# A hybrid S5 and attention decoder block on one core: y matmuls with a full-width stationary operand, and GpSimd copies back to channel order

## The chip, the cores and the metric

The kernel runs on one core of a Trainium2 chip. Its time is the device time of one execution, in microseconds (us). TensorE (PE in the rows) multiplies matrices from SBUF into PSUM; VectorE (DVE), ScalarE (ACT) and GpSimd (POOL) work on elements; SyncE (SP) issues the weight loads. Each engine takes its instructions in a fixed order and waits on semaphores of the others.

## The reference, cut to what matters

One layer of a decoder block on 256 tokens of width 2048: adaptive modulation from `c`, RMSNorm, one projection to u, q, k, v, an S5 state space mixer on u, dilated attention on q, k, v, an output projection, and a SwiGLU block. The edited work is the end of the S5 mixer: 64 groups of 16 channels with 64 complex states each.

```python
def _s5_mixer(u, a_re, a_im, log_dt, b_re, b_im, c_re, c_im, d, w_glu):
    ...
    y = (jnp.einsum('sbgn,gcn->bsgc', h_re, c_re.astype(f32))
         - jnp.einsum('sbgn,gcn->bsgc', h_im, c_im.astype(f32))
         + d.astype(f32) * uf)
    y = jax.nn.gelu(y.reshape(B, S, SSM_WIDTH))
    return y * jax.nn.sigmoid(y @ w_glu.astype(f32))
```

## The kernel before, in words

All activations are kept as a high and a low part in fp32r, and most products are three matmuls (high x high, high x low, low x high). Weights stream through a ring: `load` (line 104) has SP issue a 512 KB DMA into one of six `raw` buffers, ScalarE rounds it to `whi` (line 131), VectorE subtracts to `wlo` (line 133), and there are three pairs of those (`NHL`). The order of the loads on SP is written out by hand (lines 110 to 118); the order of the other engines' instructions is set at compile time by a scheduler that goes by priorities and by times of its own.

The S5 mixer works on 256 tokens as 64 positions j of 4 phases r. `ssm_batch(m)` (line 689) does batch m, eight groups in four partition quarters Q, for m from 0 to 7. It multiplies U with the table `wv` into S (line 698), copies S to scratch (line 701), turns it with the tables `E`, scans it along time on VectorE (line 713), turns it back into the state `hp`, and then makes y from two tables: `T` (within four tokens, from U) and `Vt` (from `hp`). In the kernel before, y has channels of quarter Q on partitions 32Q to 32Q + 31 and the phases r beside each other; every matmul has a stationary operand of 128x32, set at column 32Q of the array (lines 725 to 733). GELU follows on ScalarE and VectorE (lines 735 to 743), and lines 744 to 747 write its high and low part to `yT`, block m.

Scratch comes from `WK`: tiles of 128x3x512 with two buffers, which `ssm_batch`, `ssm_rot` (`wkr`, line 475), `ssm_tables` (`wkt`, line 502) and every other head of attention (`wkh`, line 797) share. PSUM tiles of the tag `ms` have three buffers. The batches are generators in two lanes (lines 884 to 888), of which `step` (line 865) advances some between the half blocks of the q, k, v projection (lines 889 to 906); two batches thus go nearly together. The tables of batches 6 and 7 are made between batches 2, 3 and 4, 5. After the last batch the matmuls z (line 919) read `yT`, block by block from 0 to 7, while the heads of attention and the gate1 row (memset and DMA on GpSimd, lines 253 and 254; sums on VectorE, line 268) go on.

GpSimd does memsets for tables and a few DMAs, and nothing else.

Of the kernel before, what the change touches and what calls it, by code (L numbers as in the profile page):

```python
# [7 lines left out]
F32 = mybir.dt.float32  # L8
F32R = mybir.dt.float32r
I32 = mybir.dt.int32  # L10
AF = mybir.ActivationFunctionType
ALU = mybir.AluOpType
# [49 lines left out]
def body(tc, sm, tabs, bc, brow, x, wada, wg2, win, wglu, wout, wgate, wup, wdown, out):  # L62
    nc = tc.nc
    V, A, PE, G, SP = nc.vector, nc.scalar, nc.tensor, nc.gpsimd, nc.sync
# [13 lines left out]
    def ms(shape, name="ms"):  # L78
        return ms_p.tile(shape, F32, name=name, tag="ms", bufs=3)
# [81 lines left out]
    def WK(name):  # L161

        w = p2.tile([128, 3, 512], F32, name=name, tag="wk", bufs=2)

        def part(i, *shape):
            n = math.prod(shape)
            names = "abcd"[:len(shape)]
            v = w[:, i, 0:n]
            return v.rearrange(f"p ({' '.join(names)}) -> p {' '.join(names)}", **dict(zip(names, shape)))
        return part  # L170


# [167 lines left out]
    def tt(o, a, b, op):  # L340
        V.tensor_tensor(out=o, in0=a, in1=b, op=op)  # L341
    def ts(o, a, s1_, s2_, o0, o1=None):
        if o1 is None:
            V.tensor_scalar(out=o, in0=a, scalar1=s1_, scalar2=None, op0=o0)
        else:
            V.tensor_scalar(out=o, in0=a, scalar1=s1_, scalar2=s2_, op0=o0, op1=o1)
# [121 lines left out]
    def te_parts(m):  # L468

        te = te_p[m // 2]  # L470
        T = te[:, 512 * (m % 2):512 * (m % 2) + 512].rearrange("p (q r c) -> p q r c", q=4, r=4)
        E = te[:, 1024:2048].rearrange("p (e q j) -> p e q j", e=2, q=8)
        return T, E[:, :, 4 * (m % 2):4 * (m % 2) + 4]

    def ssm_rot(mp):

        if mp == 2:
            te = xp.tile([128, D], F32, name="te", tag="x", bufs=2)
        else:
            te = p2.tile([128, D], F32, name="te", tag="te", bufs=2)  # L480
        te_p[mp] = te
        E = te[:, 1024:2048].rearrange("p (e q j) -> p e q j", e=2, q=8)
        pr = slice(8 * mp, 8 * mp + 8)
        wk = WK("wkr")
        G.memset(E[:, 0, :, 0:1], 1.0)
        G.memset(E[:, 1, :, 0:1], 0.0)
        ea, eb = wk(0, 2, 8, 32), wk(1, 2, 8, 32)
        for l in range(6):
            n = 1 << l
            for dst, r in ((ea, 0), (eb, 1)):  # L490
                f = el[:, l, r, pr].unsqueeze(1).unsqueeze(3).to_broadcast([128, 2, 8, n])
                tt(dst[:, :, :, 0:n], E[:, :, :, 0:n], f, ALU.mult)
            tt(E[:, 0, :, n:2 * n], ea[:, 0, :, 0:n], eb[:, 1, :, 0:n], ALU.subtract)
            tt(E[:, 1, :, n:2 * n], ea[:, 1, :, 0:n], eb[:, 0, :, 0:n], ALU.add)
            if l == 3:
                yield 1.5
            elif l == 4:
                yield 1.2
        rot_done.add(mp)
        yield 2.2  # L500

    def ssm_tables(m):
# [7 lines left out]
        wv_t[m] = wv  # L510
        wst = T4([128, 4, 2, 4, 32], "wst")
        wk = WK("wkt")
        T, _ = te_parts(m)
        Tf = T.rearrange("p q r c -> p (q r c)")
# [132 lines left out]
    U = xp.tile([128, 8, 4, 64], F32, name="U", tag="x", bufs=2)  # L647
# [38 lines left out]
    yT = [P8([128, 4, 2, 256], f"yT{i}", F32R) for i in range(2)]  # L686


    def ssm_batch(m):
        while m // 2 not in rot_done:  # L690
            yield None
        wv = wv_t[m]
        Vt = wv[:, 1]
        T, E = te_parts(m)
        S = ms([128, 2, 4, 64], "S")
        for Q in range(4):
            for e in range(2):
                PE.matmul(S[:, e, Q], lhsT=wv[:, 0, Q, e].rearrange("p i c -> p (i c)"), rhs=U[:, m, Q], start=True, stop=True)  # L698
        wk = WK("wks")
        a, b, s = (wk(i, 2, 4, 64) for i in range(3))  # L700
        A.copy(s, S)
        yield 0.0
        Er = E[:, 0].unsqueeze(1).to_broadcast([128, 2, 4, 64])
        Ei = E[:, 1].unsqueeze(1).to_broadcast([128, 2, 4, 64])
        tt(a, s, Er, ALU.mult)
        tt(b, s, Ei, ALU.mult)
        tt(s[:, 0], a[:, 0], b[:, 1], ALU.add)
        tt(s[:, 1], a[:, 1], b[:, 0], ALU.subtract)
        yield 2.0
        g, a2, b2 = a, b, s  # L710
        for e in range(2):
            for Q in range(4):
                V.tensor_tensor_scan(out=g[:, e, Q], data0=rho4[:, 4 * m + Q:4 * m + Q + 1].to_broadcast([128, 64]), data1=s[:, e, Q],
                                     initial=0.0, op0=ALU.mult, op1=ALU.add)
        yield 1.1
        tt(a2, g, Er, ALU.mult)
        tt(b2, g, Ei, ALU.mult)
        hp = g
        V.memset(hp[:, :, :, 0:1], 0.0)
        tt(hp[:, 0, :, 1:64], a2[:, 0, :, 0:63], b2[:, 1, :, 0:63], ALU.subtract)  # L720
        tt(hp[:, 1, :, 1:64], a2[:, 1, :, 0:63], b2[:, 0, :, 0:63], ALU.add)
        yield 2.0
        yield None
        y = ms([128, 4, 64], "y")
        for Q in range(4):
            yq = y[32 * Q:32 * Q + 32]
            for r in range(4):
                PE.matmul(yq[:, r], lhsT=T[:, Q, r], rhs=U[:, m, Q], start=r == 0, stop=False, skip_group_check=True,  # L728
                          tile_position=(0, 32 * Q))
            for r in range(4):  # L730
                for e in range(2):
                    PE.matmul(yq[:, r], lhsT=Vt[:, Q, e, r], rhs=hp[:, e, Q], start=False, stop=e == 1, skip_group_check=True,  # L732
                              tile_position=(0, 32 * Q))

        ysb, t1 = wk(1, 64, 4), wk(2, 64, 4)
        A.copy(ysb, y.rearrange("p r j -> p j r"))
        A.activation(t1, ysb, AF.Square)
        yield 0.0
        ts(t1, t1, 0.044715, 1.0, ALU.mult, ALU.add)
        tt(t1, t1, ysb, ALU.mult)  # L740
        A.activation(t1, t1, AF.Tanh, scale=math.sqrt(2.0 / math.pi))
        yield 0.6
        V.scalar_tensor_tensor(out=ysb, in0=t1, scalar=1.0, in1=ysb, op0=ALU.add, op1=ALU.mult)
        dst = yT[m // 4][:, m % 4]
        yf = ysb.rearrange("p j r -> p (j r)")
        A.mul(dst[:, 0], yf, 0.5)
        V.scalar_tensor_tensor(out=dst[:, 1], in0=yf, scalar=0.5, in1=dst[:, 0].bitcast(F32), op0=ALU.mult, op1=ALU.subtract)
        done_b.add(m)
        yield 0.7

# [133 lines left out]
    for m in BO:  # L884
        lanes[m % 2].append(ssm_batch(m))
# [24 lines left out]
    for nb in range(2):  # L910
        z = acc([128, 4, 256], "z")
        for hf in range(4):
            hl = take()
            for j in range(2):
                kc = hf * 2 + j
                for c in range(4):
                    w = slice(c * 128, c * 128 + 128)
                    for n, (wt, a) in enumerate(((hl[0], 0), (hl[0], 1), (hl[1], 0))):
                        PE.matmul(z[:, c], lhsT=wt[:, j, w], rhs=yT[kc // 4][:, kc % 4, a], start=(kc == 0 and n == 0 and c % 2 == 0),  # L919
                                  stop=(kc == 7 and n == 2), skip_group_check=True)  # L920
# [317 lines left out]
```

## Time and profile before

| | |
|---|---|
| time, median of 3 runs | 1264.25 us (1263.53 to 1267.47) |
| profiled execution | 1264.14 us |
| its span, first to last instruction | 1262.4 us |
| TensorE busy | 1216.4 us (96%), 6884 matmuls |
| VectorE busy | 790.5 us (63%) |
| ScalarE busy | 570.5 us (45%) |
| GpSimd busy | 25.2 us (2%), 50 instructions |
| chain that ended last | TensorE 80%, VectorE 9%, DMA 6%, ScalarE 3% |
| HBM read and written | 299.44 and 2.10 MB, 239 GB/s over the span |

The profile is of one execution. Times in rows are us from the start of the span, durations of single instructions are in ns where a row says min/median/max or mean. L732 is line 732 of the kernel. TensorE's durations are modelled and overlap; the start of one instruction to the start of the next is its pace. "[0.37 <-DVE yT L747]" behind an instruction means that its engine sat idle for 0.37 us before it, until that line's instruction on VectorE had ended.

### The profile page before, as it was taken

To read this page: it belongs to the slowest core of one execution; us is meant where nothing else is said; L and a number is where in the kernel's file an instruction comes from. 1 tells how busy PE (TensorE), PEld (TensorE's weight loads), DVE (VectorE), ACT (ScalarE), POOL (GpSimd) and SP (SyncE) were. 2 spreads that over 40 slices of the span, in tenths; PEclk is the share of its full clock that TensorE was granted. 3 is DMA by queue.
4 is the path that set the end of the run, shared out by engine and by line. 5 is a ranking of instruction groups with operands and counts; after the bars stand their busy time and mean duration, and the time that the engine had idled before them with its cause. 6 is when DMAs were issued, how large, how long until landed. Compare 5 with 4: busy or idle time off the path is not lost.

```text
span 1262.4 us, 18076 instructions
## 1 busy us (share of the span) xinstructions
PE 1216.4 (96%) x6884; PEld 965.2 (76%) x6884; DVE 790.5 (63%) x1389; ACT 570.5 (45%) x859; POOL 25.2 (2%) x50
## 2 busy tenths in 40 slices
PE   4888999999999999999999999999999999999998
PEld 2555667677789877688888888888888878888886
DVE  7894356667778989865655665665555444545443
ACT  3564373445455554554444444444434443333432
POOL 0210000000000000000000000000000000000000
PEclk9899999999999999999999999999999999999999
DMA  8788886777687799567777777777766556667662
GB/s 338 275 285 319 318 318 239 262 251 272 221 322 237 266 317 330 202 188 241 237 238 235 230 239 240 238 236 229 244 201 191 185 169 194 208 194 213 190 212 68
DMA packets 83032, 302.74 MB, mean 240 GB/s; under 512 B 9248, under 2 KB 9664, under 8 KB 82304
## 3 DMA queue, kind: packets, MB, share of 16 engines
q1 hardware_dynamic: 80784, 294.69, 70.4%
q10 hardware_dynamic: 1728, 4.38, 0.9%
q0 software_dynamic: 432, 2.51, 0.5%
q8 instruction: 54, 0.88, 0.3%
q14 instruction: 34, 0.28, 0.1%
HBM read 299.44 MB, written 2.10 MB: 239 GB/s over the span
## 4 chain that ended last, share of the span: by engine, by line
PE 80%; DVE 9%; DMA 6%; ACT 3%; issue 2%; SPq 0%; DVEq 0%; ACTq 0%
PE ff L150 38%; PE dn L150 14%; PE qkv L150 8%; PE dnl L150 5%; DMA raw<-wada 3%; PE ada L231 3%; PE uacc L608 3%; DVE wlo L133 2%; PE y L732 2%; DMA raw<-win 1%; DVE gate L268 1%; PE q L150 1%; PE y L728 1%; PE z L919 1%; PE S L698 1%
## 5 line engine op out<-in xcount | busy, mean ns | idle before, releaser
L133 DVE TENSOR_TENSOR wlo<-raw,whi 128x1024 fp32r<-128x1024 f32 x365 | 445.7, 1223 | 325.8 <-ACT whi L131 325.0
L131 ACT CAST whi<-raw 128x1024 fp32r<-128x1024 f32 x365 | 384.4, 1053 | 511.1 <-PE ff L150 268.6
L150 PE MATMUL ff<-whi,h2T 128*128 128x512 f32 x1408 | 437.2, 390 | 0.7 <-DVE h2T L1034 0.5
L150 PEld LDWEIGHTS ff<-whi,h2T 128*128 128x128 f32 x1408 | 264.0, 188 | 56.8 <-DVE h2T L1034 0.9
L150 PE MATMUL ff<-wlo,h2T 128*128 128x512 f32 x704 | 274.1, 389 | 0.0
L150 PE MATMUL dn<-whi,aT 128*128 128x512 f32 x528 | 163.4, 390 | 0.0
L150 PEld LDWEIGHTS ff<-wlo,h2T 128*128 128x128 f32 x704 | 132.2, 188 | 27.1
L150 PEld LDWEIGHTS dn<-whi,aT 128*128 128x128 f32 x528 | 99.1, 188 | 21.1 <-ACT whi L131 0.2
L150 PE MATMUL qkv<-whi,hT 128*128 128x512 f32 x320 | 107.4, 402 | 0.1
L150 PE MATMUL dn<-wlo,aT 128*128 128x512 f32 x264 | 103.1, 391 | 0.0
L231 PE MATMUL ada<-raw,c 128*4 128x256 f32 (+1 forms) x736 | 68.9, 470 | 16.1 <-DVE c L179 9.5
L150 PEld LDWEIGHTS qkv<-whi,hT 128*128 128x128 f32 x320 | 59.8, 188 | 25.1 <-issue 9.0
L1092 DVE SCALAR_TENSOR_TENSOR gate<-raw,cs,gate 128x1024 f32<-128x1024 f32 x32 | 41.1, 1285 | 56.5 <-DMA raw<-wg 56.5
L608 PE MATMUL uacc<-hT,whi 128*128 128x256 f32 x256 | 55.0, 308 | 9.4 <-ACT whi L131 4.9
L150 PE MATMUL qkv<-wlo,hT 128*128 128x512 f32 x160 | 63.6, 397 | 0.4 <-DVE wlo L133 0.4
L608 PEld LDWEIGHTS uacc<-hT,whi 128*128 128x128 f32 x256 | 42.5, 202 | 21.2 <-issue 9.5
L150 PEld LDWEIGHTS dn<-wlo,aT 128*128 128x128 f32 x264 | 49.6, 188 | 10.6 <-issue 0.5
L150 PE MATMUL dnl<-whi,aT 128*128 128x512 f32 x176 | 54.4, 389 | 0.0
L268 DVE SCALAR_TENSOR_TENSOR gate<-raw,cs,gate 128x512 f32<-128x512 f32 x64 | 47.8, 749 | 6.7 <-DMA raw<-wada 5.8
L231 PEld LDWEIGHTS ada<-raw,c 128*4 128x4 f32 x736 | 13.9, 87 | 42.5 <-issue 14.7
L608 PE MATMUL uacc<-hT,wlo 128*128 128x256 f32 x128 | 38.3, 300 | 1.1 <-DVE wlo L133 0.8
L150 PEld LDWEIGHTS dnl<-whi,aT 128*128 128x128 f32 x176 | 33.0, 188 | 7.0 <-DVE o L341 0.2
(312 smaller groups left out, 1262.1 us busy)
## 6 DMA issues: line engine op xcount, KB each, us to landing
raw<-wada SPq DMA_DIRECT2D x160, 512.0 KB, 5.3
raw<-wgate SPq DMA_DIRECT2D x88, 512.0 KB, 4.5
raw<-wup SPq DMA_DIRECT2D x88, 512.0 KB, 4.3
raw<-wdown SPq DMA_DIRECT2D x88, 512.0 KB, 4.3
raw<-win SPq DMA_DIRECT2D x64, 512.0 KB, 5.4
raw<-wout SPq DMA_DIRECT2D x32, 512.0 KB, 4.8
raw<-wg SPq DMA_DIRECT2D x32, 512.0 KB, 4.3
raw<-wglu SPq DMA_DIRECT2D x8, 512.0 KB, 4.8
```

The costliest lines, as they stand in the source:

```text
L131: A.copy(hi, raw)
L133: V.tensor_tensor(out=lo, in0=raw, in1=hi.bitcast(F32), op=ALU.subtract)
L150: PE.matmul(ps[t] if type(ps) is list else ps[:, t], lhsT=lhs(a, t), rhs=w[:, j], start=first and n == 0, stop=last and n == 2)
L231: PE.matmul(ps[32 * q:32 * q + 4, 0:w], lhsT=c7[:, kc, 3 - i:7 - i], rhs=wts[t][:, j * w:(j + 1) * w], start=q not in seen, stop=n == len( ...
L268: V.scalar_tensor_tensor(out=gb, in0=wt[:, j], scalar=cs[:, 2 * h + j:2 * h + j + 1], in1=gb, op0=ALU.mult, op1=ALU.add)
L608: PE.matmul(uacc[b][:, c], lhsT=wt[:, j, w], rhs=h[:, j, a], start=(kc == 0 and n == 0 and c % 2 == 0), stop=(kc == 15 and n == 2), skip_g ...
L698: PE.matmul(S[:, e, Q], lhsT=wv[:, 0, Q, e].rearrange("p i c -> p (i c)"), rhs=U[:, m, Q], start=True, stop=True)
L728: PE.matmul(yq[:, r], lhsT=T[:, Q, r], rhs=U[:, m, Q], start=r == 0, stop=False, skip_group_check=True, tile_position=(0, 32 * Q))
L732: PE.matmul(yq[:, r], lhsT=Vt[:, Q, e, r], rhs=hp[:, e, Q], start=False, stop=e == 1, skip_group_check=True, tile_position=(0, 32 * Q))
L919: PE.matmul(z[:, c], lhsT=wt[:, j, w], rhs=yT[kc // 4][:, kc % 4, a], start=(kc == 0 and n == 0 and c % 2 == 0), stop=(kc == 7 and n == 2) ...
L1092: V.scalar_tensor_tensor(out=g, in0=wt, scalar=cs[:, k:k + 1], in1=g, op0=ALU.mult, op1=ALU.add)
```

## The change

y is made with the full 128 columns of the array: `T[:, Q]` and `Vt[:, Q, e]` are taken with all four phases at once as a stationary operand of 128x128, so there are 12 matmuls in a batch for 48. y then has (phase r, channel) on partitions and (Q, j) along them. GELU runs in that layout. Its high part and low part, which were written to `yT`, go to scratch, and 16 copies on GpSimd bring them to `yT`: each takes the 32 partitions of a phase r, columns of quarter Q, both parts, and writes them to the 32 partitions of Q, at every fourth column. The batch's scratch tile is now read last by these copies.

```diff
+        part.w = w
         return part
...
         y = ms([128, 4, 64], "y")
         for Q in range(4):
-            yq = y[32 * Q:32 * Q + 32]
-            for r in range(4):
-                PE.matmul(yq[:, r], lhsT=T[:, Q, r], rhs=U[:, m, Q], start=r == 0, stop=False, skip_group_check=True,
-                          tile_position=(0, 32 * Q))
-            for r in range(4):
-                for e in range(2):
-                    PE.matmul(yq[:, r], lhsT=Vt[:, Q, e, r], rhs=hp[:, e, Q], start=False, stop=e == 1, skip_group_check=True,
-                              tile_position=(0, 32 * Q))
-
-        ysb, t1 = wk(1, 64, 4), wk(2, 64, 4)
-        A.copy(ysb, y.rearrange("p r j -> p j r"))
+            PE.matmul(y[:, Q], lhsT=T[:, Q].rearrange("p r c -> p (r c)"), rhs=U[:, m, Q], start=Q == 0, stop=False, skip_group_check=True)
+            for e in range(2):
+                PE.matmul(y[:, Q], lhsT=Vt[:, Q, e].rearrange("p r c -> p (r c)"), rhs=hp[:, e, Q], start=False, stop=e == 1,
+                          skip_group_check=True)
+
+        ysb, t1 = wk(2, 4, 64), wk(1, 4, 64)
+        A.copy(ysb, y)
...
-        dst = yT[m // 4][:, m % 4]
-        yf = ysb.rearrange("p j r -> p (j r)")
-        A.mul(dst[:, 0], yf, 0.5)
-        V.scalar_tensor_tensor(out=dst[:, 1], in0=yf, scalar=0.5, in1=dst[:, 0].bitcast(F32), op0=ALU.mult, op1=ALU.subtract)
+        hi, lo = wk(0, 4, 64), wk(1, 4, 64)
+        A.mul(hi.bitcast(F32R), ysb, 0.5)
+        V.scalar_tensor_tensor(out=lo, in0=ysb, scalar=0.5, in1=hi, op0=ALU.mult, op1=ALU.subtract)
+
+        dst = yT[m // 4][:, m % 4].rearrange("p a (j r) -> p a j r", r=4)
+        for Q in range(4):
+            for r in range(4):
+                G.tensor_copy(dst[32 * Q:32 * Q + 32, :, :, r], wk.w[32 * r:32 * r + 32, 0:2, 64 * Q:64 * Q + 64])
         done_b.add(m)
```

## Rows read from the trace of the kernel before

**Rows 1.** Windows: stretch, its length, busy us (instructions) of each engine, clock, DMA.
```profile
190.00:386.00 196.00, 195.01 (x1627) 145.57 (x1626) 133.97 (x350) 92.23 (x213) 8.08 (x13) 1.00 0.73 261
386.00:401.00 15.00, 15.00 (x124) 14.83 (x123) 13.90 (x33) 9.14 (x16) 0.00 (x0) 1.00 0.79 250
401.00:440.00 39.00, 39.00 (x227) 33.53 (x226) 38.00 (x68) 23.00 (x37) 0.00 (x0) 1.00 0.76 251
```
**Rows 2.** Waits of TensorE, 190 to 401 us: total, times, longest.
```profile
PE pk L560 <- ACT te L558: 0.9, 1, 0.9
```
**Rows 3.** Tile y: line, engine, operation, count, ns min/median/max, first and last start, form.
```profile
L732 PE MATMUL y<-wks,wv x512: 219/219/243, 201.8 to 376.7; 128*32 128x64 f32 x171
...
L728 PE MATMUL y<-U,te x256: 219/219/244, 201.3 to 375.8; 128*32 128x64 f32 x128
```
**Rows 4.** Chain that ended last, 250 to 560 us: start, length, what.
```profile
253.13 0.44 PE y L728 x8
...
262.49 2.95 PE qkv L150 x12
```
**Rows 5.** Timeline of TensorE: start, length, line, operation, out and in, form, count.
```profile
222.26 2.00 PE L698 MATMUL S<-U,wv 128*128 128x64 f32 x16
224.06 0.48 PE L150 MATMUL qkv<-whi,hT 128*128 128x512 f32 x1
```
**Rows 6.** Tile yT, its two writers.
```profile
L746 ACT ACTIVATE yT<-wks x8: 405/420/429, 222.4 to 379.9; 128x256 fp32r<-128x256 f32 x8
L747 DVE SCALAR_TENSOR_TENSOR yT<-wks,yT x8: 418/419/427, 222.9 to 380.4; 128x256 fp32r<-128x256 f32 x8
```
**Rows 7.** Groups of GpSimd: busy us, mean ns of one | idle before.
```profile
L519 POOL MEMSET wst<- 128x1024 f32 x8 | 7.6, 955 | 72.8 <-PE pk L556 45.7 <-PE qtp L784 19.7 <-DVE bct L341 7.3
...
L517 POOL MEMSET te<- 128x256 f32 x8 | 2.2, 310 | 0.0
L253 POOL MEMSET gate<- 128x2048 f32 x1 | 1.8, 1809 | 75.4 <-PE y L732 75.4
```
**Rows 8.** Line 573, a copy between partition quarters of SBUF on ScalarE.
```profile
L573 ACT COPY te<-te x24: 293/296/301, 62.6 to 298.0; 32x128 f32<-32x128 f32 x24
```
**Rows 9.** Timeline of ScalarE, two first uses of a scratch buffer.
```profile
269.10 0.39 ACT L532 COPY wkt<-bct 128x64 f32<-128x64 f32 x2 [0.69 <-DVE yT L747]
...
322.88 0.58 ACT L701 COPY wks<-S 128x512 f32<-128x512 f32 x1 [0.37 <-DVE yT L747]
```
**Rows 10.** Timeline of VectorE, end of the second pair of batches.
```profile
265.23 0.42 DVE L747 SCALAR_TENSOR_TENSOR yT<-wks,yT 128x256 fp32r<-128x256 f32 x1
...
268.64 0.42 DVE L747 SCALAR_TENSOR_TENSOR yT<-wks,yT 128x256 fp32r<-128x256 f32 x1
```
**Rows 11.** Timeline of VectorE, the state hp of batch 5.
```profile
312.48 0.41 DVE L341 TENSOR_TENSOR wks<-wks 128x252 f32<-128x252 f32 x1
```
**Rows 12.** Timeline of TensorE, y of the third pair begins.
```profile
309.03 0.61 PE L728 MATMUL y<-U,te 128*32 128x64 f32 x8
```
**Rows 13.** Timeline of VectorE, the last pair, and the gate row's first sum.
```profile
379.81 0.42 DVE L747 SCALAR_TENSOR_TENSOR yT<-wks,yT 128x256 fp32r<-128x256 f32 x1
...
385.72 1.53 DVE L268 SCALAR_TENSOR_TENSOR gate<-raw,cs,gate 128x512 f32<-128x512 f32 x2
```
**Rows 14.** Timeline of TensorE, z begins to read blocks 6 and 7 of yT.
```profile
397.05 0.48 PE L919 MATMUL z<-yT,whi 128*128 128x256 f32 x2
...
399.20 0.40 PE L919 MATMUL z<-yT,whi 128*128 128x256 f32 x2
```
**Rows 15.** Timeline of GpSimd, four memsets of the tables.
```profile
33.28 3.61 POOL L520 MEMSET wv<- 128x1024 f32 x4
```
**Rows 16.** Timeline of VectorE in the same time.
```profile
33.85 1.22 DVE L133 TENSOR_TENSOR wlo<-raw,whi 128x1024 fp32r<-128x1024 f32 x1
```
**Rows 17.** Line 346, the tensor_scalar that makes htmp: ns min/median/max, first and last start.
```profile
L346 DVE TENSOR_SCALAR htmp<-xnT,g,sh x16: 395/411/2057, 35.0 to 162.0; 128x256 f32<-128x256 f32 x16
```
**Rows 18.** DMA issues, 190 to 386 us: issuer, count, size, us from issue to landing.
```profile
gate<-brow POOLq DMA_DIRECT2D x1, 8.0 KB, 2.4
```

## The prediction

> **What bounds the kernel now.** I read the windows first, to find which engine is full in the stage that holds the edited work; then the waits of TensorE there; then the price of each instruction that goes or comes; last the hand-overs behind which new work is queued. The edit lies where `ssm_batch` runs, from 190 to 386 us. There TensorE is busy for 195.0 of 196 us, VectorE for 134.0, ScalarE for 92.2 and GpSimd for 8.1, and the DMA engines have a share of 0.73; from 401 us on VectorE is the full one, with 38.0 of 39 us [rows 1]. What matters is that TensorE's own waits between 190 and 401 us come to one of 0.9 us [rows 2]. So in this stage nearly every microsecond that TensorE is spared moves the end, as long as its operands arrive. The stage behind starts from what this one leaves: its weights come in the order written out for SP, as ring slots come free, so it moves with the first stage unless VectorE is given more work there.
>
> **TensorE: what goes.** Over eight batches the y matmuls are 256 + 512 = 768 instructions (each fp32 matmul is two) [rows 3], 96 a batch. Their modelled 219 ns overlap, so I take the pace: two batches run together from 253.13 until the next qkv matmul at 262.49 us, 9.36 us for 192, or 48.8 ns each [rows 4]. The y work is 768 x 48.8 ns = 37.4 us.
>
> **TensorE: what comes.** Per batch 4 T and 8 Vt matmuls, again two instructions each: 24, or 192 in all. They have a stationary operand of 128x128 and 64 moving columns, which is the form of the S matmuls (L698) of the same batches. Sixteen of those run from 222.26 to 224.06 us: 112.5 ns each [rows 5]. So 192 x 112.5 ns = 21.6 us, and TensorE is spared 37.4 - 21.6 = **15.8 us**, about 2 us a batch. This is the solid term: both paces are of the same data, buffers and stage.
>
> **ScalarE and VectorE.** The chain from y to yT keeps the number, engine and size of its instructions: the copy, two activations and final scaling on ScalarE, four operations on VectorE. `hi` and `lo` go to scratch instead of yT; scaling and subtraction cost 0.42 us each as now [rows 6]. That is nothing either way.
>
> **GpSimd: what comes.** 16 copies a batch, 128 in all, each 32 partitions by 2x64 elements, with its write spread at every fourth element. The trace has no GpSimd instruction that reads SBUF, so I bound one copy. GpSimd's memsets take 0.31 us for 256 columns and 0.95 us for 1024 [rows 7]: 0.84 ns a column, so 128 columns cost 0.31 - 0.11 = 0.20 us. That is the low end, for it only writes. The nearest row in kind is ScalarE's copy of 32x128 from one partition quarter of SBUF to another, 0.30 us [rows 8]; twice that, 0.60 us, is my high end, for a slower reader or for the spread write. I take c = 0.30 us, the row that is nearest: 4.8 us a batch, 9.6 us a pair, 38 us in all on an engine that has 188 us free. Throughput is no question; what waits for the copies is. The Trainium skill (GPSIMD Engine Reference, section 3.1) gives about 1.8 cycles an element at 1.2 GHz for a tight loop; an estimate from that page is 128 x 1.8 / 1.2 = 0.19 us a copy, and the sum below would be about 1250 us by it. No run here shows it.
>
> **Who waits for the copies.** First, scratch: WK has two buffers, and a batch now keeps its own until its sixteen copies have read it. Today the next user starts as soon as the last subtraction ends: ScalarE's wkt copy at 269.10 and the S copy at 322.88 us both wait for L747 [rows 9]. ScalarE and VectorE work in order, so weight splits (L131, L133) and the scratch chains queue behind such a waiting instruction. Batches 2 and 3 end their L747 at 265.65 and 269.06 us [rows 10]; 32 copies from 265.65 free the second buffer 32c - 3.4 us later than now, 6.2 us at c = 0.30. The tables and batches 4 and 5 behind it shift by that; their S tiles stay longer in PSUM, which has three buffers for such (ms). What is late next is y of the second batch of that pair: its input is ready at 312.89 us [rows 11], TensorE begins the pair at 309.03 [rows 12], so by the pace above the second y begins at 313.7 at the earliest: 0.8 us to spare, and 2 us less once the first y is shorter. It is then late by 32c - 3.4 - 0.8 + 2.0 = 32c - 2.2, or 7.4 us. TensorE has split weights for up to three half blocks (NHL) to run meanwhile, so between none and all of it shows; I take half, 3.7 us (range 0 to 7.4).
>
> Second, z: the last pair ends its first L747 at 380.23 us [rows 13], and z first reads row blocks 6 and 7 at 397.05 and 399.20 [rows 14]. 32 copies fit into these 19.0 us up to c = 0.59; at 0.30 they end at 389.8, so this costs nothing.
>
> Third, GpSimd's queue: the table memsets and the memset and DMA of the gate1 row. A table memset behind a pair's copies waits 9.6 us at most, which is part of the scratch term. The gate row is read by VectorE from 385.72 us on [rows 13]; it stays free if its memset is queued ahead of the last copies, as its buffer comes free before they can start.
>
> **Sum.** 15.8 - 3.7 = 12.1 us. The profiled execution took 1264.14 us (span 1262.4 and 1.7 around it), 0.1 below the median, 1264.25. Forecast: 1264.1 - 12.1 = **1252 us**. Within this case, c from 0.20 to 0.60 gives 15.8 - 2.1 to 15.8 - 8.5 - 0.2, or 1250.4 to 1257 us.
>
> **Rivals.** (A) All of it: TensorE always has weights to run while the pair is late. 1264.1 - 15.8 = 1248 us. For it: no wait over 0.9 us now; against: in-order ScalarE.
>
> (B) GpSimd and VectorE block each other. The trace has the beginning of this: while GpSimd wrote four memsets from 33.28 to 36.89 us, a 128x256 tensor_scalar (median 0.41 us) that began at 35.0 took 2.06 us, while a 128x1024 subtraction inside the same time took its usual 1.22 [rows 15 to 17]. So some VectorE forms wait out a GpSimd instruction, and two-input ones do not wait for a memset; whether they wait for a copy, which reads, no row shows. If they take turns, a copy waits for VectorE in 134 of 196 us, for a mean instruction of 134.0/350 = 0.38 us: c becomes 0.30 + 0.68 x 0.38 = 0.56. The scratch term is (32 x 0.56 - 2.2)/2 = 7.9 us; the last copies run to 398 us, some 22 of them beside a VectorE that is full from 386 us on, where they cost it 22 x 0.30 = 6.6 us. 15.8 - 14.5 leaves 1.3: 1263 us, no change. The Trainium skill (SBUF — State Buffer, Who interferes with whom) states just this: a VectorE instruction with two SBUF inputs contends with a GpSimd instruction that reads SBUF, the second to start being fully blocked. The rows with memsets agree with its other half.
>
> (C) Slower: the copies are long. Place: the two hand-overs above. Price: (32c - 2.2)/2 + (32c - 19.0). It eats the 15.8 us at c = 0.75; at c = 1.0 it is 14.9 + 13.0 and the kernel takes 1276 us. For it: nothing bounds a read, cross-quarter, spread-write copy on GpSimd from above; against: both nearest rows are at a third of this.
>
> (D) The gain comes back elsewhere: the gate row's memset is queued behind the last copies (380.2 + 9.6 + 1.8 of memset [rows 7] + 2.4 of DMA [rows 18] = 394.0, 8.3 us after VectorE wants it), or the DMA engines, at 0.73 x 196/180 = 0.79, hold TensorE up now and then. About 1261 us.
>
> **How the numbers follow.** Forecast 0.46, A 0.14, B 0.16, C 0.14, D 0.10. A measurement here can tell 0.3%, 3.8 us, from no change, so faster is below 1260.4. Faster: 0.46 + 0.14 and a fifth or so of B and D, 0.66. Slower (above 1268): C and a little of B, 0.16. Same: 0.18. The range takes in A with 2 us for the paces, and B, D and C up to c = 0.85 (15.8 - 12.5 - 8.2, or 1269): 1246 to 1270 us; the upper part of C and a little below are left out.
>
> **What would show it.** The y matmuls: 64 and 128 instructions, a batch in 2.7 us against 4.7; with more than 3.2 the solid term is wrong. GpSimd's copies spaced at 0.20 to 0.60 us; at 0.75 or more C holds. If VectorE's subtractions (1.22 us) or the 0.42 us ones lengthen while copies run, B holds. TensorE idle before y or in front of z, or ScalarE's S and wkt copies waiting for GpSimd, size the scratch term. If TensorE has no new waits and z still begins less than 8 us earlier, the premise that TensorE bounds this stage is wrong.

## The result, and the profile after

The changed kernel takes 1284.43 us (median of 4 runs, 1283.8 to 1287.3), beside 1264.42 us for the kernel before on the same chip: a ratio of 1.016, interval 1.0136 to 1.0185. It is 20 us **slower**; the forecast was 1252 us and its range ended at 1270. The profiled span is 1282.0 us against 1262.4. Lines of the kernel after stand one higher or up to four lower than before (S copy L702, y L727 and L729, `hi` L742, `lo` L743, the copies L748, z L920).

The windows come first, as they did before [rows 1]. Columns: stretch, its length, busy us and instructions of PE, PEld, DVE, ACT and POOL, granted clock, DMA share, GB/s. The last three rows are parts of the first two stretches.

```profile
190.00:386.00 196.00, 175.03 (x998) 126.55 (x991) 125.76 (x334) 86.20 (x202) 53.47 (x109) 0.93 0.68 246
401.00:440.00 39.00, 31.53 (x216) 29.35 (x215) 31.00 (x62) 20.14 (x34) 11.41 (x18) 0.87 0.57 176
220.00:235.00 15.00, 10.78 (x48) 7.51 (x46) 8.05 (x24) 5.52 (x25) 11.04 (x24) 0.82 0.59 200
280.00:295.00 15.00, 9.76 (x47) 8.01 (x48) 14.44 (x48) 8.78 (x18) 1.02 (x3) 0.52 0.24 72
401.00:420.00 19.00, 11.53 (x81) 11.11 (x79) 11.01 (x27) 6.13 (x12) 11.41 (x18) 0.73 0.48 158
```

TensorE, busy for 195.0 of these 196 us before, now idles for 21 of them, and VectorE and ScalarE are less busy too: all three wait for something. Their waits between 180 and 430 us name it (engine and line, what released it: total, times, longest). First TensorE's own, then the others that wait for the copies:

```profile
PE wtp L551 <- issue: 10.7, 1, 10.7
PE z L920 <- POOL yT L748: 7.5, 1, 7.5
PE qkv L150 <- DVE wlo L133: 6.6, 6, 1.9
PE qkv L150 <- ACT whi L131: 3.6, 2, 2.3
```
```profile
ACT wks L702 <- POOL yT L748: 23.2, 4, 6.7
...
DVE wkr L342 <- POOL yT L748: 12.2, 1, 12.2
...
ACT wkt L533 <- POOL yT L748: 10.9, 1, 10.9
```

Where there was one wait of 0.9 us [rows 2] there are these four, 28.4 us, at three kinds of place: the tables behind the second pair (wtp, wkt, wkr), the S copies behind the other pairs, and z. The first and last use of the qkv and z tiles on TensorE give the sum: the qkv stage was 181.8 to 385.8 and is 178.9 to 394.2 us, 11.3 us longer where 15.8 less was wanted; z was 386.5 to 414.6 and is 394.9 to 432.5, 9.5 us longer. 11.3 + 9.5 less 2.9 for the earlier start, and 1.7 in other places, are the 19.6 us of the span.

GpSimd's timeline has the copies themselves (start, length of the run, line, operation, out and in, form, count, idle before and what ended it):

```profile
214.57 8.14 POOL L748 CAST yT<-wks 32x128 fp32r<-32x128 f32 x16
225.71 8.83 POOL L748 CAST yT<-wks 32x128 fp32r<-32x128 f32 x16 [3.00 <-DVE wks L743]
...
265.38 15.27 POOL L748 CAST yT<-wks 32x128 fp32r<-32x128 f32 x32 [2.96 <-DVE wks L743]
...
332.92 17.55 POOL L748 CAST yT<-wks 32x128 fp32r<-32x128 f32 x32 [22.85 <-DVE wks L743]
...
391.93 21.23 POOL L748 CAST yT<-wks 32x128 fp32r<-32x128 f32 x32 [5.51 <-DVE wks L743]
```

The pace of a copy, the length of a run over its copies, is 0.48 us in the second pair, 0.55 in the third, 0.66 in the last, where the forecast had 0.30. What they hold up is seen in three timelines behind the second pair, whose 32 copies end at 280.65 us. VectorE and ScalarE:

```profile
279.75 0.37 DVE L342 TENSOR_TENSOR wkr<-te,el 128x16 f32<-128x16 f32 x2 [12.23 <-POOL yT L748]
```
```profile
280.68 0.39 ACT L533 COPY wkt<-bct 128x64 f32<-128x64 f32 x2 [10.86 <-POOL yT L748]
283.48 1.25 ACT L535 COPY wst<-wkt 64x512 f32<-64x512 f32 x2 [2.42 <-DVE wkt L342]
284.75 1.05 ACT L131 CAST whi<-raw 128x1024 fp32r<-128x1024 f32 x1
```

And TensorE in the same time:

```profile
273.12 1.04 PE L232 MATMUL ada<-raw,c 128*4 128x512 f32 x8
284.83 1.94 PE L551 MATMUL wtp<-smt,wst 128*128 128x128 f32 x8 [10.66 <-issue]
...
288.45 1.81 PE L699 MATMUL S<-U,wv 128*128 128x64 f32 x8
```

The tables stand at the head of three in-order queues. ScalarE's wkt copy and VectorE's first wkr product wait for the scratch buffer, so neither splits a weight; and TensorE's next instruction is wtp, which needs wst, which needs wkt. It would have stood still with any number of split weights in reserve. After the idle 10.66 us its granted clock is 0.52 over 280 to 295 us, nearly all of it the lower level, 1.2 GHz, where the stretches of [rows 1] were at 1.00: eight S matmuls take 1.81 us, 226 ns each, against 112.5 before [rows 5].

### The profile page after: what moved, and what is told of

It reads as the page before. It is cut to its first block, busy times and chain, and to the rows that moved or that the text cites. A ratio compares the mean times of both kernels' runs of the same rounds, so it can differ in the third digit from the quotient of the medians.

```text
span 1282.0 us, 17054 instructions
## 1 busy us (share of the span) xinstructions
PE 1208.9 (94%) x6308; PEld 955.5 (75%) x6308; DVE 792.2 (62%) x1389; ACT 570.4 (44%) x859; POOL 91.1 (7%) x178
## 4 chain that ended last, share of the span: by engine, by line
PE 77%; DVE 8%; POOL 5%; DMA 4%; ACT 4%; issue 3%; DVEq 0%; ACTq 0%; POOLq 0%
PE ff L150 37%; PE dn L150 14%; PE qkv L150 6%; POOL yT L748 5%; PE dnl L150 5%; PE wo L150 3%; PE uacc L609 2%; PE ada L232 2%; DVE wlo L133 2%; DMA raw<-wada 2%; DMA raw<-win 1%; PE z L920 1%; ACT whi L131 1%; PE q L150 1%; PE y L729 1%
## 5 line engine op out<-in xcount | busy, mean ns | idle before, releaser
L131 ACT CAST whi<-raw 128x1024 fp32r<-128x1024 f32 x365 | 384.2, 1053 | 508.4 <-PE ff L150 268.6
L150 PE MATMUL ff<-whi,h2T 128*128 128x512 f32 x1408 | 438.6, 391 | 0.7 <-DVE h2T L1035 0.5
L150 PEld LDWEIGHTS ff<-whi,h2T 128*128 128x128 f32 x1408 | 264.4, 188 | 56.7 <-ACT h2T L1034 1.2
L150 PE MATMUL ff<-wlo,h2T 128*128 128x512 f32 x704 | 274.3, 390 | 0.0
L150 PE MATMUL dn<-whi,aT 128*128 128x512 f32 x528 | 163.3, 390 | 0.0
L150 PEld LDWEIGHTS ff<-wlo,h2T 128*128 128x128 f32 x704 | 132.5, 188 | 27.1
L150 PEld LDWEIGHTS dn<-whi,aT 128*128 128x128 f32 x528 | 99.1, 188 | 20.9 <-ACT whi L131 0.2
L150 PE MATMUL qkv<-whi,hT 128*128 128x512 f32 x320 | 111.1, 415 | 3.7 <-ACT whi L131 3.6
L150 PE MATMUL dn<-wlo,aT 128*128 128x512 f32 x264 | 103.1, 391 | 0.0
L150 PEld LDWEIGHTS qkv<-whi,hT 128*128 128x128 f32 x320 | 62.5, 196 | 30.2 <-ACT whi L131 9.7
L150 PE MATMUL qkv<-wlo,hT 128*128 128x512 f32 x160 | 66.4, 415 | 6.6 <-DVE wlo L133 6.6
L1093 DVE SCALAR_TENSOR_TENSOR gate<-raw,cs,gate 128x1024 f32<-128x1024 f32 x32 | 41.1, 1284 | 44.7 <-DMA raw<-wg 44.7
L748 POOL CAST yT<-wks 32x128 fp32r<-32x128 f32 x128 | 65.7, 513 | 39.7 <-DVE wks L743 34.3
L150 PEld LDWEIGHTS dn<-wlo,aT 128*128 128x128 f32 x264 | 49.6, 188 | 10.8 <-issue 0.5
L150 PE MATMUL dnl<-whi,aT 128*128 128x512 f32 x176 | 54.4, 389 | 0.0
L232 PEld LDWEIGHTS ada<-raw,c 128*4 128x4 f32 x736 | 13.8, 87 | 42.2 <-issue 14.1
L150 PEld LDWEIGHTS qkv<-wlo,hT 128*128 128x128 f32 x160 | 31.5, 197 | 15.1 <-DVE wlo L133 8.3
```

The lines of the kernel that those rows point to most:

```text
L131: A.copy(hi, raw)
L150: PE.matmul(ps[t] if type(ps) is list else ps[:, t], lhsT=lhs(a, t), rhs=w[:, j], start=first and n == 0, stop=last and n == 2)
L232: PE.matmul(ps[32 * q:32 * q + 4, 0:w], lhsT=c7[:, kc, 3 - i:7 - i], rhs=wts[t][:, j * w:(j + 1) * w], start=q not in seen, stop=n == len( ...
L748: G.tensor_copy(dst[32 * Q:32 * Q + 32, :, :, r], wk.w[32 * r:32 * r + 32, 0:2, 64 * Q:64 * Q + 64])
L1093: V.scalar_tensor_tensor(out=g, in0=wt, scalar=cs[:, k:k + 1], in1=g, op0=ALU.mult, op1=ALU.add)
```

## The experiments

The theory after the result: the premise and the y term hold, and the copies cost what they cost only through three hand-overs, the scratch behind the second pair, the scratch behind the others, and z. Its rivals: that the quick y gains less than its count says; that GpSimd and VectorE slow each other down wherever they meet; that a copy which crosses partition quarters is what is long; that the number of copies and a changed order cost the time, not their length. Before is 1264.46, 1265.27, 1264.73 or 1263.65 us in the groups of runs below, and every ratio is to the one of its own group.

**1. The y part alone.**

```diff
-        hi, lo = wk(0, 4, 64), wk(1, 4, 64)
-        A.mul(hi.bitcast(F32R), ysb, 0.5)
...
+        A.mul(dst[:, 0], yf, 0.5)
+        V.scalar_tensor_tensor(out=dst[:, 1], in0=yf, ...
```

> The y part alone: y is made with the 128-wide stationary operand, and the two GELU parts are written straight to yT in (phase, channel) order, without the 16 GpSimd copies of a batch (so z reads its rows in another order: the reordering is left out). If TensorE bounds this stage, as the forecast had it, the kernel is some 15.8 us faster than before: about 1249 us (1246 to 1252). If the premise was wrong and TensorE's time comes back as waits for weights, 1258 us or more.

Measured: 1248.15 us, ratio 0.9868 (0.9841 to 0.9895). The step that was called solid is: 16.3 us gained, 15.8 forecast. In its profile, of an execution of 1252.79 us, the qkv stage is 182.9 to 369.8 us, 186.9 long against 204.0, and TensorE's waits from 180 to 400 us are 1.7 us in all:

```profile
PE qkv L150 <- DVE wlo L133: 0.8, 2, 0.4
PE S L699 <- ACT wks L702: 0.6, 1, 0.6
PE qkv L150 <- ACT whi L131: 0.3, 1, 0.3
```

So the copies, and the hand-overs that they lengthen, cost 1284.4 - 1248.2 = 36.3 us. That sum is what the other runs divide.

**2. The copies alone.** The y matmuls of before, and copies from scratch that stay on their partitions.

```diff
-                G.tensor_copy(..., wk.w[32 * r:32 * r + 32, 0:2, 64 * Q:64 * Q + 64])
+                G.tensor_copy(..., wk.w[32 * Q:32 * Q + 32, 0:2, 64 * r:64 * r + 64])
```

> The copies alone: the kernel before with its narrow y matmuls, and the parts in the scratch tile, from which 16 GpSimd copies a batch of the same size and spread bring them to yT; they stay on the same 32 partitions. If the cost of the changed kernel is that of the copies alone, this takes 1284 + 15.8 = about 1300 us (1292 to 1304). If crossing from one quarter of the partitions to another is what makes a copy long, copies here take 0.30 us or less in place of 0.41 and the time is 1285 or less.

Measured: 1280.97 us, 1.0126 (1.0099 to 1.0153). The expectation was too high: here the copies cost 16.5 us, not 36. The tile's row of yT (count, ns min/median/max, first and last start):

```profile
L752 POOL CAST yT<-wks x128: 400/412/2307, 220.4 to 409.2; 32x128 fp32r<-32x128 f32 x128
```

The record of one copy is as long as in the changed kernel (399/408), yet the runs are shorter, 11.32 us for the 32 of the second pair against 15.27, and the wtp wait is 2.1 us against 10.7. Copies follow one another faster here. Two rows of GpSimd's timeline where VectorE is idle but for 0.2 us or less, of this run and of the changed kernel:

```profile
274.78 3.44 POOL L752 CAST yT<-wks 32x128 fp32r<-32x128 f32 x11
```
```profile
267.65 11.61 POOL L748 CAST yT<-wks 32x128 fp32r<-32x128 f32 x26
```

Eleven copies of 0.41 us in 3.44 us overlap; 26 in 11.61 us do not. Where nothing holds them up, a copy of this run starts 0.265 us after the one before while both keep to one quarter, and 0.45 us after it at every fourth copy, where Q changes; eight such short steps, two long ones and the last copy are the 3.44 us. In the changed kernel each copy reads another quarter than the one before, and the step is 0.45 us throughout such stretches, though the quarter that is written stays for four copies. So the expectation's second case, 0.30 us or less and a time of 1285 or less, came true for the step and the time, and not for the length of a record: 24 steps that are 0.18 us shorter are 4.3 us, about the 4.0 between the two runs of 32. It is the change of quarter between one copy and the next that goes with the longer step; a copy that crosses quarters, but reads the same one as the copy before, was not run.

The copies of this run hold scratch for less time than those of the changed kernel, so their 16.5 us are not the price of the same copies. Nor does it price y that this run takes 3.5 us less than the changed kernel: the two differ in the copies too, and the intervals overlap.

**3. The write in a row.** The copies write 64 elements side by side instead of every fourth.

```diff
-        dst = yT[m // 4][:, m % 4].rearrange("p a (j r) -> p a j r", r=4)
+        dst = yT[m // 4][:, m % 4].rearrange("p a (r j) -> p a j r", r=4)
```

> The changed kernel with copies that write 64 elements in a row in place of every fourth (the order of tokens in yT is another, so the product that follows is of other tokens: one size of the copy is changed, not its count). If the spread write is what makes a copy take 0.41 us, copies take 0.20 to 0.30 us here and the kernel about 1270 us; if the fixed part or the reading is, they stay at 0.38 us or more and the kernel within 5 us of 1284.

Measured: 1271.77 us, 1.0066 (1.0042 to 1.0091). Row of yT and TensorE's largest waits:

```profile
L748 POOL CAST yT<-wks x128: 281/292/1368, 214.4 to 399.8; 32x128 fp32r<-32x128 f32 x128
```
```profile
PE wtp L551 <- issue: 7.1, 1, 7.1
...
PE z L920 <- POOL yT L748: 5.0, 1, 5.0
```

The spread write is 0.115 us of a copy's 0.41. Cutting it gives back 12.7 us: 0.115 x 128 is 14.7 us of GpSimd time, so nearly all of what GpSimd spares reaches the end.

**4. A stage of its own.** The parts of batches 0 to 5 wait for their copies in the block of yT that belongs to batch m + 2, which nothing uses yet, and not in scratch. Number and size of the copies stay.

```diff
+        if m < 6:
+            st = yT[(m + 2) // 4][:, (m + 2) % 4]
...
+            hl = st.bitcast(F32)
...
-                G.tensor_copy(..., wk.w[32 * r:32 * r + 32, 0:2, 64 * Q:64 * Q + 64])
+                G.tensor_copy(..., hl[32 * r:32 * r + 32, :, 64 * Q:64 * Q + 64])
```

> The changed kernel, but the parts of batches 0 to 5 are staged in the yT block of the batch two later, which nobody has written yet, in place of the scratch tile; so the scratch tile is free as soon as the state and GELU are done, and the same 128 copies run. Theory H (hand-over): the loss is TensorE's idle time behind ScalarE's and VectorE's instructions that wait for scratch, about 20 us of it and the slower clock after it; then this takes about 1257 us (1250 to 1263), with the wait of z for the last copies (7.5 us) left. Theory L (the copies and VectorE block each other, wherever the parts are staged): it stays within 8 us of the changed kernel, 1276 us or more.

Measured: 1260.07 us, 0.9958 (0.9937 to 0.9978): 24.4 us back. TensorE's waits from 180 to 410 us, and the copies:

```profile
PE z L928 <- POOL yT L756: 7.5, 1, 7.5
PE qkv L150 <- DVE wlo L133: 2.5, 5, 0.8
PE S L699 <- ACT wks L702: 0.6, 1, 0.6
```
```profile
216.04 21.14 POOL L756 CAST yT<-yT 32x128 fp32r<-32x128 f32 x32 [0.75 <-DVE yT L745]
...
366.51 21.23 POOL L756 CAST yT<-wks 32x128 fp32r<-32x128 f32 x32 [5.51 <-DVE wks L750]
```

All scratch waits are gone and the z wait is as it was. The copies of the first pair run for 21.1 us here, longer than in the changed kernel (8.14 + 8.83); the qkv stage is 179.7 to 368.8 us, 189.1 long against 186.9 with no copies at all. So by these two profiles 96 slow copies that nobody waits for cost this stage 2.2 us; by the medians of run 1 and of run 6, where the z wait is gone too, it is 5.3 us at most. That bounds what GpSimd and VectorE do to each other there. z is 369.5 to 407.9 us, 38.4 us against 28.0 in run 1.

**5. A stage for the second pair only**, the edit of run 4 for batches 2 and 3.

```diff
+        if m in (2, 3):
+            st = yT[(m + 2) // 4][:, (m + 2) % 4]
```

> The changed kernel with only batches 2 and 3 staged in yT; behind them the tables of batches 6 and 7 take the scratch tiles, and there the changed kernel has its longest waits (VectorE 12.2 us, ScalarE 10.9 us, TensorE 10.7 us idle). Hand-over theory: those go, with the slower clock behind them, and the waits behind the first and third pair stay: 1284 - 13 = about 1271 us (1267 to 1275). If the three hand-overs are one delay that is passed on, all 24 us go (1260) or nearly none (1280).

Measured: 1271.35 us, 1.0047 (1.0031 to 1.0064). The wkr, wkt and wtp waits are gone; these remain:

```profile
ACT wks L702 <- POOL yT L756: 22.9, 4, 6.7
...
PE z L928 <- POOL yT L756: 7.5, 1, 7.5
...
PE qkv L150 <- DVE wlo L133: 7.4, 7, 1.9
```

So, as the hand-over theory had it, the 24.4 us split into 13.1 for the hand-over to the tables and 11.3 for the S copies behind the other pairs, which the forecast had at nothing.

**6. The last pair's copies on three engines**, GpSimd, ScalarE and VectorE in turn, once on top of run 4 and once alone.

```diff
-                G.tensor_copy(...
+                (G.tensor_copy if m < 6 else (G.tensor_copy, A.copy, V.tensor_copy)[(4 * Q + r) % 3])(...
```

> Parts staged in yT as in e2_own_stage, and of the last two batches' 32 copies a third each goes to GpSimd, ScalarE and VectorE, so that they end before z reads blocks 6 and 7. e2_own_stage left z with 7.5 us of waiting and took 38.4 us for z against 28.0 without copies. Hand-over theory: this takes 1260 - 10 = about 1250 us (1247 to 1254), within 3 us of the kernel without any copies, which ran 1248. If GpSimd's copies cost VectorE time by themselves, whoever waits, it stays at 1256 or more.

> The changed kernel (parts in the scratch tile, which the copies hold) with only the last two batches' copies shared among GpSimd, ScalarE and VectorE. The wait of z (7.5 us, and the slower clock behind it) should go, the scratch waits of the three pairs before stay: 1284 - 10 = about 1274 us (1271 to 1277). If the tail and the scratch waits cover each other, less than 5 us.

Measured: with the stage 1253.40 us, 0.9904 (0.9876 to 0.9932), 6.7 us better than without; alone 1278.35 us, 1.0101 (1.0068 to 1.0135), 6.1 us better than the changed kernel, where 10 was expected. The z wait is gone in both, and z takes 29.2 us (369.5 to 398.7) and 28.8 us. In the profile of the second, z is 8.8 us shorter than in the changed kernel's, but the qkv stage starts 4.5 us later, ahead of all that this edit touches; why is not shown. The tail is a term of 6 to 7 us, and adds to the scratch term.

**7. All copies on ScalarE.**

```diff
-                G.tensor_copy(...
+                A.copy(...
```

> The changed kernel with all 128 copies on ScalarE in place of GpSimd, from the scratch tile. At the 0.30 us of its copies of 32x128 (line 573 of before) a batch takes 4.8 us of ScalarE, which has 112 of 196 us free, and the copies no longer meet VectorE at a shared port. If what hurts is the length of the hand-over, it falls from 8 to 10 us to 5 us a batch: about 1260 us (1254 to 1266). If ScalarE's queue, which also splits the weights, is then what TensorE waits for, 1270 or more.

Measured: 1274.71 us, 1.0072 (1.0041 to 1.0103). A copy takes 414 ns on ScalarE too, so the row taken for c, 0.30 us [rows 8], was no match even on its own engine: that one writes its elements in a row, and where run 11 has ScalarE make these copies so, they take 297 ns. The second case of the expectation came true; TensorE's waits changed their owner:

```profile
PE qkv L150 <- ACT whi L131: 12.1, 4, 7.7
PE z L920 <- ACT whi L131: 6.0, 1, 6.0
```

**8. The early copies twice**, on top of run 4: 96 copies more, in no one's way by the theory.

```diff
-        for Q in range(4):
+        for Q in [0, 1, 2, 3] * (2 if m < 6 else 1):
```

> e2_own_stage with every copy of batches 0 to 5 made twice (same source, same place): 96 more GpSimd copies while nobody waits for scratch. Hand-over theory: a copy costs only what waits for it, and nothing waits for these before z: 1258 to 1264 us, against 1260 for e2_own_stage. Blocking theory: 96 copies more, each of which holds VectorE up or is held up by it, cost what the first 96 did; if that is 0.1 to 0.2 us each on the path, 1270 us or more.

Measured: 1278.67 us, 1.0101 (1.0063 to 1.0140), 18.6 us slower than run 4. By its number this is the case of the blocking theory, 1270 or more, and the hand-over theory's 1258 to 1264 failed. The trace tells them apart: VectorE's subtractions have their usual median, 1.225 us as in run 4, and one new wait carries nearly all of it, `PE qkv L150 <- ACT whi L131: 17.5, 1, 17.5`. Timelines of GpSimd and of ScalarE:

```profile
261.94 34.81 POOL L756 CAST yT<-yT 32x128 fp32r<-32x128 f32 x64
296.82 0.42 POOL L563 MEMSET te<- 128x384 f32 x1
```
```profile
297.27 0.60 ACT L574 COPY te<-te 32x128 f32<-32x128 f32 x2 [18.49 <-POOL te L563]
297.89 1.04 ACT L131 CAST whi<-raw 128x1024 fp32r<-128x1024 f32 x1
```

A table memset of 0.42 us stood behind 64 copies on GpSimd, ScalarE's table copy behind the memset, and the next weight split behind that copy. It is the hand-over that the forecast named third, harmless with 32 copies and not with 64: copies that nobody reads cost what is queued behind them.

**9. The same hold without copies.** Run 1, and eight memsets a batch over two scratch parts that are done with, a hold of 7.6 us or so a batch.

```diff
+        for _ in range(8):
+            G.memset(wk.w[:, 1:3], 0.0)
```

> The y part alone as in e1_no_copies (z reads its rows in another order: the reordering is left out), and in place of a batch's copies eight GpSimd memsets of 128x1024 over two thirds of its scratch tile, 0.95 us each, 7.6 us a batch, which hold the tile as long as the copies did. A memset reads nothing, and in the trace of before a two-input VectorE instruction ran at its usual length beside one. Hand-over theory: the scratch waits of the changed kernel come back without any copy, 1248 + 24 = about 1270 us (1264 to 1276), z without a wait. If the loss is that copies and VectorE block each other, it stays at 1248 to 1255.

Measured: 1260.52 us, 0.9964 (0.9948 to 0.9981), 12.4 us slower than run 1, between the two expectations. The waits for the held scratch are short:

```profile
ACT wks L702 <- POOL wks L746: 4.7, 2, 2.3
...
ACT wkt L533 <- POOL wks L746: 3.6, 1, 3.6
```

Here the order written at compile time came out otherwise: ScalarE's S copy stands behind other work instead of ahead of weight splits. And the memsets hold up VectorE's tensor_scalars. Two of them, in VectorE's timeline, and TensorE's wait behind the first:

```profile
221.70 6.84 DVE L347 TENSOR_SCALAR ssq<-ssq 128x8 f32<-128x8 f32 x1 [1.38 <-ACT qsq L763]
...
378.67 9.30 DVE L345 TENSOR_SCALAR ast<-ast 128x2 f32<-128x2 f32 x1
```
```profile
232.36 0.79 PE L150 MATMUL qkv<-wlo,hT 128*128 128x512 f32 x1 [6.21 <-DVE wlo L133]
```

The median of either is 0.17 us; the second ends at 387.97 us, where the last series of memsets ends. ScalarE waits 11.4 us behind the first and 8.3 behind the second, and TensorE's two long waits stand behind them: 6.2 us for a weight split and 5.2 for a head of attention (`PE ptp L828 <- ACT hd L825: 5.2, 1, 5.2`). No wait of TensorE is behind the held scratch. So by this trace the loss is for the most part that of memsets which hold VectorE up, and the run was no test of the hold: it neither supports the hand-over theory nor speaks against it.

**10. Copies a quarter as long.** The number of copies and their hold on scratch stay.

```diff
+                G.tensor_copy(dst[32 * Q:32 * Q + 32, :, 0:16, r],
+                              wk.w[32 * r:32 * r + 32, 1:3, 64 * Q:64 * Q + 16])
```

> The changed kernel with all its copies, GpSimd's order and the scratch hold kept, but each copy only a quarter as long: ScalarE and VectorE write the two parts straight to yT, and GpSimd then copies 2x16 instead of 2x64 elements from the scratch of the same batch over them (the reordering of the other elements is left out). One copy should fall from 0.41 us to between 0.11 and 0.25 us, a pair's 32 copies from 15 to 21 us to 4 to 9. Theory one, the length of the copies sets the price: the line through the two lengths measured (0.41 us, 1284.4 us, and 0.29 us, 1271.8 us: 105 us for each us of a copy) gives 1252 us at 0.11 and 1267 us at 0.25, and never under the 1248.2 us without copies; wkt and wkr wait for at most 5 us each and the z wait is gone. Theory two, the number of copies and the later order of the hand-over set it, whatever their length: 1265 us or more, with ScalarE's S copies still waiting over 3 us each for GpSimd.

Measured: 1267.33 us, 1.0024 (1.0005 to 1.0043). Row of yT:

```profile
L748 POOL CAST yT<-wks x128: 230/238/1252, 214.8 to 393.1; 32x32 fp32r<-32x32 f32 x128
```

A quarter of the elements takes 0.238 of 0.408 us: 0.170 us for 96 elements is 1.8 ns an element, over a fixed part of 0.18 us. Both are of the write at every fourth element. With the changed kernel and run 3 the price of a copy's median length can be read: 1284.4 us at 0.408, 1271.8 at 0.292, 1267.3 at 0.238, some 100 us for each us of c. Theory one's line gives 1266 for the last, so the time follows the length, and by an estimate from the same line the gain over before is gone at about c = 0.2. But the run doesn't decide between the theories as they were put, for its 1267.3 us fit theory two's "1265 us or more" as well. By their size the waits speak for either: wtp waits 0.8 us, but wkt still 9.4, two S copies 4.5 and 4.8, as theory two had it, and z 3.4 where none was expected. The runs of 32 copies didn't shrink to the 4 to 9 us expected; they took 9.9, 13.0 and 17.2 us. So a part of the loss that goes with the number of copies, each with its fixed part, stays.

**11. A version from these findings.** Run 4's stage, run 6's tail, and run 3's write in a row, with z computed in phase order and its two parts put back into token order behind it.

```diff
+        dst = yT[m // 4][:, m % 4].rearrange("p a (r j) -> p a j r", r=4)
...
+            A.mul(mv[0][:, c], yv[:, c], 0.5)
```

> e5_stage_and_tail with copies that write 64 elements in a row: yT and z keep tokens phase by phase, and the two operations that make the mixS halves write them back in token order (in four pieces each). Copies take 0.28 us by themselves, as in e4_dense_write, against 0.41, so 96 of them take some 12 us less of GpSimd; with nobody waiting for them the hand-over theory gives no more than 0 to 3 us: 1250 to 1254. If what is left over the kernel without copies (5 us) is the copies' meeting with VectorE, it falls by a third to a half: 1249 to 1251.

Measured: 1249.07 us, 0.9879 (0.9857 to 0.9901): 15.7 us faster than before, 35 faster than the change as made, and within 1 us of run 1, which has no copies. TensorE waits for no copy. The 4.3 us to run 6 are less sure: the intervals of the two ratios overlap, and in the two profiles, of executions of 1253.33 and 1254.08 us, qkv and z are together 1.7 us shorter.

## Why the prediction was wrong

**The premise and the y term were right.** TensorE bounds the stage, and y gives 16.3 us (15.8 forecast) when nothing is behind it. The arithmetic chain costs nothing, as said; the gate row's memset runs at 382.98 us, ahead of the last copies, as said, and no wait of TensorE there names a DMA, so rival D fell; and rival A's 1248 is what runs 1 and 11 reach.

**The 36.3 us of the copies, divided:** 24.4 at the scratch hand-overs (run 4; 13.1 behind the second pair, 11.3 behind the others, run 5), 6.7 at z (run 6), 5.3 left. Of the last, 4.3 go with the write in a row by the medians (run 11). The forecast had 3.7, 0 and 0.

**The copy's length c was mis-sized.** Taken at 0.30 from [rows 8], it is 0.41 by the record of one copy, and 0.45 from one start to the next, which is what 32c counts. The write at every fourth element makes 0.115 of that (run 3), and I had put it into the high end and then not used it; the change of quarter from copy to copy makes 0.18 of the step (run 2), and I had not thought of it: the chosen row was near in size and engine, not in the write, and on its own engine the real copy takes 0.41 too (run 7). The Trainium skill (GPSIMD Engine Reference, section 3.1) would have it at 0.19 by the estimate in the prediction; its 1.8 cycles at 1.2 GHz are 1.5 ns an element. For the spread write run 10 shows 1.8 ns over a fixed 0.18 us, and the estimate lacked the fixed part; for the write in a row, if its fixed part is the same, run 3's 0.292 us leave 0.9 ns.

In place it is longer still. Groups of GpSimd from 268 to 279 us, where VectorE is idle, and from 402 to 410, where it is busy for 7.96 of 8 us:

```profile
L748 POOL CAST yT<-wks 32x128 fp32r<-32x128 f32 x26 | 10.5, 405 | 1.1
```
```profile
L748 POOL CAST yT<-wks 32x128 fp32r<-32x128 f32 x9 | 7.8, 872 | 0.4
```

That is rival B's mechanism, and the trace agrees with the Trainium skill's rule (SBUF — State Buffer, Who interferes with whom): most of VectorE's work in the second stretch has two SBUF inputs. But its price was put in the wrong place. VectorE's subtractions keep their 1.21 to 1.29 us in the second stretch; the copies lose, which matters where somebody waits for them, and costs 2.2 to 5.3 us where nobody does (run 4).

**The scratch term failed by its factor and its place.** At the measured pace of 0.477 its 32c - 2.2 is 13.1 us, and run 5 gives 13.1 us for that hand-over; the equal figures are luck. The forecast counted how late the second y of the next pair would be, and TensorE has no wait before any y; what it has is 10.7 us before wtp, and the slower clock behind that. I took half of the lateness, on the ground that TensorE has split weights to run meanwhile. It had not the choice: wtp stood at the head of its own queue, and the splits of later weights behind wkt and wkr on the other two. The wait of the tables became idle time of VectorE, ScalarE and TensorE alike, 12.2, 10.9 and 10.7 us. And the term was priced once, behind the second pair, since only there had I looked for a consumer with little to spare; the S copies behind the other pairs wait 23.2 us on ScalarE, ahead of weight splits, and that is 11.3 us more.

**The z term failed by two rows.** 32 copies were to fit into 19.0 us up to c = 0.59, from a start at 380.2 [rows 13]. They ran at 0.66, beside a full VectorE, and they began late: VectorE does the last pair's first subtraction 6.1 us after TensorE's last y matmul (385.3), where it was 3.1 us before, 376.7 [rows 3] to 379.81 [rows 13]; a weight split that waits for ScalarE now stands ahead of it:

```profile
388.25 0.42 DVE L740 SCALAR_TENSOR_TENSOR wks<-wks 128x256 f32<-128x256 f32 x1
390.31 1.23 DVE L133 TENSOR_TENSOR wlo<-raw,whi 128x1024 fp32r<-128x1024 f32 x1 [1.64 <-ACT whi L131]
391.45 0.42 DVE L743 SCALAR_TENSOR_TENSOR wks<-wks 128x256 f32<-128x256 f32 x1
```

**Rival C had the mechanism and the two places, and the wrong price.** It put the turning point at c = 0.75 and 16 to 48 us on each us of c. The runs put it near 0.2, or 0.25 by the step from start to start, and the slope near 100 (run 10): with three hand-overs instead of one, all of the lateness instead of half, and TensorE at the lower clock behind each. With its own c = 0.30, but the whole 7.4 us at the second pair and the others in the proportion of run 5, the scratch term would be, by an estimate, 7.4 x 24.4 / 13.1 = 13.8 us, and 2 of the 15.8 us are left: no change, from that one step.

**What stays open.** How much of the loss is the slower clock was not measured by itself: TensorE's waits from 180 to 430 us are 29.4 us in the changed kernel (the four above and 1.0 in two short ones) and 1.7 in run 1; the loss is 36.3, and the 8.6 us between are what is left for the clock and for all else. Nor is it shown why the compile-time order in run 9 differed, what a hold on scratch without copies costs, or whether copies in an order that keeps the quarter read would have made the change pay.

## What to carry to other kernels

When work moves to an idle engine, price not its throughput but the buffer that it holds: list every next user of that buffer, see whether that user stands at the head of an in-order queue, and charge the whole lateness at each one, because what is queued behind it, on TensorE too, cannot overtake. Give the moved copies a buffer with no near user and share the last of them, which are read at once, among engines: here that turned 1284 us into 1253, and a write in a row into 1249. For the length of an unseen instruction, match the row's access pattern, the write's above all, before its engine and size, and count the step from start to start, not the length of one record: it was 0.265 or 0.45 us for the same 0.41.

## What the runs showed of the hardware

- A GpSimd copy of 32x128 fp32 with a write at every fourth element takes 0.41 us, in a row 0.29; ScalarE takes 0.41 for the same spread copy, against 0.30 for the copy in a row of [rows 8]. The record is as long when source and target are the same quarter (400/412 ns in run 2), but the step to the next copy is not: 0.265 us while copies keep to one quarter, 0.45 where the next reads another.
- A GpSimd copy takes 405 ns beside an idle VectorE and 872 beside a full one, while VectorE hardly lengthens. GpSimd's memsets do the reverse: a 128x2 tensor_scalar took 9.30 us and a 128x8 one 6.84, against medians of 0.17, each through a series of memsets of 0.95 us (run 9), as the 2.06 us one had hinted [rows 17].
- Behind 10.7 us of idle time TensorE's granted clock was 0.52 over a stretch of 15 us, and 64-column matmuls took 226 ns instead of 112.5.
